# Layer 0's FFN in a two-layer backbone: the first product's copy, the left sums, row loads and residual loads in another order

## The chip, the core and the metric

The kernel runs on one core of one Trainium2 chip. The metric is the device time of one execution in microseconds (us); the figure that counts is the median of the runs. All data are fp32. The engines are TensorE (PE: matmuls; its weight loads are listed apart as PEld), VectorE (DVE), ScalarE (ACT), GpSimd (POOL) and SyncE (SP, which issues nearly all DMAs here). Each engine executes its own instructions strictly in the order in which they were written, and an instruction that has to wait holds up all that stand behind it on its engine.

## The reference

Two layers act on 1024 latent and 256 context tokens of width 1024. Layer 0 mixes by pooling, layer 1 by attention; behind each stands a gated ConvFFN. Every sub-layer is a root-mean-square norm with shift, scale and gate taken from a conditioning vector `c` through `ada_w`:

```
sh1, sc1, g1, sh2, sc2, g2 = split(silu(c) @ ada_w[i] + ada_b[i], 6)
x = x + g1 * mixer(modulate(rmsnorm(x), sh1, sc1))
x = x + g2 * conv_ffn(modulate(rmsnorm(x), sh2, sc2))

def conv_ffn(h):                        # D_FF = 2816 = 22 x 128
    u = h @ w_up                        # (tokens, 5632)
    u = u[t-1]*cw[0] + u[t]*cw[1] + u[t+1]*cw[2] + cb
    a, v = split(u, 2)
    return (silu(a) * v) @ w_down
```

The context stream runs through the same weights with a modulation of its own.

## The kernel before

**Products.** To keep fp32 accuracy a product is made of three matmuls: each operand is split into a high part (line 162, a cast on ACT) and a low part (line 163, a subtraction on DVE or POOL), and `mm3` (lines 166 to 168) multiplies high by high, high by low and low by high. For the latents, the up and the down product of layer 0 are done in Strassen's manner, with 7 half-size products in place of 8, so sums of weights and of tokens have to be made beforehand.

**Before the FFN.** The residual stream after the pool mixer, `tm(i)` for 128 tokens each (i = 0 to 7 latent, 8 and 9 context), is normalised: `norm2(i)` writes `xh2[i]`, on ACT (line 484) or on DVE (line 486). `turn_h2` transposes a piece on PE (line 795), and ACT (line 804) and DVE (line 803) read the transposed piece from PSUM, applying scale and shift (columns of `mod`, made on DVE in line 340). Lines 442 and 443 finish the mixer's output for other tiles. Up to the middle of this stretch a scheduler orders the instructions by due times and its own estimates; behind `tc.manual_schedule()` the order is that of a list of due times alone: `acts` holds (time, function) pairs, and `play` writes them between the PE's items as the estimated PE time goes by.

**Token sums.** `t0_subs` (line 818, DVE) makes four sums of the latent tokens in place, `t0_hi` (line 821, ACT) casts each, `t0_lo` (line 824, DVE) makes its low part. The four lie as halves of two tensors (`feat0`).

**Up phase.** 22 steps j, each one a block of 128 gate and 128 value columns of `w_up`. A step j >= 2 has 7 latent products of 512 columns (numbered 1 to 7) and four of 256 columns for the context (Ga, Gb, Va, Vb), in the order 1, 6, 2, Ga, Gb, 5, 7, 3, Va, 4, Vb. Product 1's bank is copied to SBUF by ACT (line 755, "the copy"), and product 2 goes on accumulating in that bank, so product 2 waits for the copy. DVE adds the products up (line 710). The convolution of the latent gate is an `ident` on ACT (line 717), two taps on DVE (line 722) and a silu on ACT (line 726); the value has the ident and the taps; the context has both in a smaller form (256 columns). Line 733 multiplies gate and value and the result is stored to `g0_d[j]`. POOL makes the weight sums of the coming step (line 660) and low parts.

**Left sums.** For the down phase, sums of pairs of `w_down` blocks (stored to `tw0_d`) and of pairs of gated blocks (stored to `sg0_d`) are made by groups of two loads (line 593), four DVE operations (line 590) and two stores (line 596). Of the 22 groups one falls to each up step from j = 3 on, and 3 are left for the beginning of the down phase.

**Down phase.** The context product goes first (22 blocks f, each with 4 `mm3`, some 2.7 us), then products 1, 6, 2 and so on with 11 blocks each. Each block's weights and gated values are loaded by SP (lines 947 and 951) into a ring of 4 buffers, cast by ACT, and their low parts are made by DVE or POOL. In the same time SP loads 24 row blocks of layer 1's `ada_w` (line 1023, 512 KB each) into a ring of 6; 16 of them are multiplied on PE by `c` (line 1033), 8 on DVE. The context's output leaves its banks on DVE (line 994) after its residual has been loaded (line 984). The first row group on PE (line 1033) writes a bank that line 994 has to read first.

Of the kernel before, what the change touches and what calls it, by code (L numbers as in the profile page):

```python
# [20 lines left out]
KT = D // P  # L21
LAT = 1024
# [60 lines left out]
def backbone(ctx: ExitStack, tc: tile.TileContext, io, out: bass.AP):  # L83
# [465 lines left out]
    on(73, lambda: rstd_of(0, 4))  # L549
    on(73.1, *(lambda i=i: norm2(i, True) for i in range(4)))  # L550

# [57 lines left out]
    def side_sums(w_dn, g_d, tw_d, sg_d, swap):  # L609
# [15 lines left out]
    w_up0 = io["ffn_w_up"][0].rearrange("(k p) f -> p k f", p=P)  # L625
    feat0 = {0: at(176, KT, 512), 512: at(192, KT, 512)}
    flo0 = {0: at(176, KT, 512, r=True), 512: at(192, KT, 512, r=True)}
    t_f32 = (feat0[0][:, :HK], feat0[512][:, HK:], feat0[512][:, :HK], feat0[0][:, HK:])
    t_sp = [(at(o, HK, 512, r=True), lo) for o, lo in
            zip((136, 104, 144, 96), (flo0[0][:, :HK], flo0[512][:, HK:], flo0[512][:, :HK], flo0[0][:, HK:]))]  # L630

# [103 lines left out]

    def ctx_acts(j, tg, tv):
        r = timed(tg, (0.1, 0.6, 1.0, 1.5), conv_ops(0, j, 0, csc[0], ctx_ps(j, 0), CTX))
        r += timed(tv, (0.1, 0.6, 1.0), conv_ops(0, j, 1, csc[1], ctx_ps(j, 1), CTX))
        return r + [(tv + 1.6, lambda: gated(j, *csc, LAT))]

    def lat_acts(j, t12, t21, tg, silu=3.8):
# [3 lines left out]
        r += timed(t21, (0.9, 1.9, 2.9), conv_ops(0, j, 1, cs[1], psum[:, v : v + LAT], LAT))  # L745
        return r + [(tg, lambda: gated(j, *cs, 0))]

    def up0_acts(j, end):
        b = banks0(j)
        b0, b1, bx, b2, b3 = (bank(n) for n in (b[1], b[3], 6, 4, 5))  # L750
        t12 = max(end[j, 3], end[j, 5] + 0.75) + 0.05
        t21 = max(end[j, 4] + 0.05, t12 + 2.85)
        tg = max(t21 + 4.1, end.get((j + 1, 6), 0) + 0.1)
        sums = [
            (end[j, 1] - 0.06, lambda: nc.scalar.copy(s1c0[j % 2], b0)),
            (end[j, 6], lambda: plus(vsum0, bx, s1c0[j % 2])),
            (end[j, 5], lambda: plus(rsum0, bx, s1c0[j % 2])),
            (end[j, 7], lambda: plus(b3, b2, rsum0)),
            (t12, lambda: plus(b1, b1, rsum0)),
            (t21, lambda: plus(b2, b2, vsum0)),  # L760
        ]
        return sums + lat_acts(j, t12, t21, tg) + ctx_acts(j, end[j, "Gb"], end[j, "Vb"])

# [27 lines left out]
    def turn_h2(o, kt, pt):  # L791
        n = 512 if o < LAT else CTX
        a = o // P
        for q in range(n // P):
            nc.tensor.transpose(pt[:, q * P : (q + 1) * P], xh2[a + q][:, kt * P : (kt + 1) * P], ident)
        s = 0 if o < LAT else 1
        sc, sh = mod[:, 0, 4, s, kt : kt + 1], mod[:, 0, 3, s, kt : kt + 1]
        hi, lo = h2_at(o, kt)
        f = feat0[o][:, kt] if o < LAT else hfr()
# [13 lines left out]
    def t0_subs(q):  # L813

        b11, b21 = feat0[0][:, q], feat0[0][:, HK + q]
        b12, b22 = feat0[512][:, q], feat0[512][:, HK + q]
        for o, x, y in ((b11, b12, b11), (b12, b22, b12), (b22, b22, b11), (b21, b21, b22)):
            nc.vector.tensor_tensor(out=o, in0=x, in1=y, op=ALU.subtract)
# [53 lines left out]
    for j, p in order:  # L872
        put(step0(j, p), j, p)
    acts = [(1, lambda: rstd_of(4, NLT))] + [(2, lambda i=i: norm2(i, i > 5)) for i in range(4, NLT)]

# [4 lines left out]
    for j, t in ((0, end0), (1, end1)):  # L880
        acts += ctx_acts(j, end[j, "Gb"], end[j, "Vb"]) + lat_acts(j, t - 0.7 + 1.3 * j, t - 0.7, t + 4 + 6 * j, 3.8 + 4.5 * j)
    acts += [(t_raw + 0.1 * n, lambda op=op: w0_make(1, op)) for n, op in enumerate(PLAIN)]
# [22 lines left out]

    for j in range(3, NJ):
        acts += sums0_acts(j - 3, end[j - 1, 7] + 0.1, end[j, 6] + 0.15, 0.01, end[j, 6] + 7)

# [1020 lines left out]
```

## Time and profile before

| | us |
|---|---|
| median of three runs (2240.66, 2245.22, 2245.85) | 2245.22 |
| the profiled execution | 2237.87 |
| its span, from first to last instruction | 2235.7 |
| PE busy in the span (10972 matmuls) | 2150.6 (96%) |
| DVE / POOL / ACT busy | 1514.5 / 1333.7 / 1000.6 |

Matmuls overlap, so PE's lost time is read from the distances of their starts. The chain of work that ended last gives PE 51%, DVE 21%, ACT 8% and POOL 7% of the span. By stage: the tokens' norm and transposes run from about 90 to 152 us, the up phase of layer 0 from there to about 690, its down phase to about 1000, layer 1 after that.

### The profile page before, as it was taken

What the parts mean: (1) busy time and instruction counts of PE and PEld (TensorE: products, weight loads), DVE (VectorE), ACT (ScalarE), POOL (GpSimd) and SP (SyncE); (2) the same over time, 40 slices, a digit from 0 to 9 for tenths busy, and PEclk for the clock granted to TensorE, in tenths of its full rate; (3) what the DMA queues carried; (4) which work ended last, traced back from release to release, by engine and by line L of the source; (5) the groups of instructions that cost most, each with busy time, mean ns of one, the idle gap of its engine ahead of it and who ended that gap; (6) DMA issues with size and microseconds to landing.
All of it is one profiled execution on the core that took longest, in us unless ns stands there. A gap on an engine that the chain in (4) does not pass through costs nothing.

```text
span 2235.7 us, 30177 instructions
## 1 busy us (share of the span) xinstructions
PE 2150.6 (96%) x10972; PEld 1768.7 (79%) x10972; DVE 1514.5 (68%) x2097; ACT 1000.6 (45%) x1589; POOL 1333.7 (60%) x881
## 2 busy tenths in 40 slices
PE   6899999999999899999998999989999999999999
PEld 5677888888887677887876877878878888888887
DVE  6666776777768657687776666746766666667565
ACT  5364333333335343454446665644443433444442
POOL 0444777677773267773345776734487777774755
PEclk9999999999999999999999999999999999999999
DMA  9832445444447998651000212123145555559775
GB/s 330 309 99 78 149 156 167 144 139 146 160 157 246 341 319 288 203 180 59 33 22 10 76 57 75 49 76 95 57 139 191 191 189 189 193 198 326 248 241 183
DMA packets 213927, 363.78 MB, mean 163 GB/s; under 512 B 15106, under 2 KB 114066, under 8 KB 213778
## 3 DMA queue, kind: packets, MB, share of 16 engines
q1 hardware_dynamic: 213778, 361.85, 47.7%
q8 instruction: 86, 1.41, 0.3%
q14 instruction: 63, 0.52, 0.1%
HBM read 271.86 MB, written 89.93 MB: 162 GB/s over the span
## 4 chain that ended last, share of the span: by engine, by line
PE 51%; DVE 21%; issue 8%; ACT 8%; POOL 7%; DMA 4%; SPq 0%; ACTq 0%; POOLq 0%; DVEq 0%
PE psum L166 15%; PE psum L167 15%; PE psum L168 15%; DVE a L722 5%; DVE a L590 5%; POOL a_512r L163 3%; PE psum L1390 3%; ACT a L717 2%; POOL a L660 2%; ACT a_512r L162 2%; DVE a_512r L163 1%; DVE a L1372 1%; DVE a L1217 1%; DVE a L733 1%; PE psum L315 1%
## 5 line engine op out<-in xcount | busy, mean ns | idle before, releaser
L163 POOL TENSOR_TENSOR a_512r<-a,a_512r 128x512 fp32r<-128x512 f32 x353 | 521.9, 1490 | 374.6 <-ACT a_512r L162 372.6
L162 ACT CAST a_512r<-a 128x512 fp32r<-128x512 f32 x507 | 294.2, 618 | 427.3 <-POOL a L660 200.7
L166 PE MATMUL psum<-a_2048r,a_512r 128*128 128x256 f32 (+1 forms) x1120 | 400.3, 358 | 7.1 <-DVE a L722 2.9
L168 PE MATMUL psum<-a_2048r,a_512r 128*128 128x256 f32 (+1 forms) x1120 | 399.0, 356 | 0.0
L167 PE MATMUL psum<-a_2048r,a_512r 128*128 128x512 f32 (+1 forms) x800 | 274.9, 344 | 0.0
L163 DVE TENSOR_TENSOR a_512r<-a,a_512r 128x512 fp32r<-128x512 f32 x154 | 180.6, 1182 | 110.7 <-ACT a_512r L162 108.5
L166 PEld LDWEIGHTS psum<-a_2048r,a_512r 128*128 128x128 f32 x1120 | 212.4, 190 | 41.0 <-DVE psum L1631 2.9
L166 PE MATMUL psum<-a_512r 128*128 128x512 f32 x616 | 242.9, 394 | 0.0
L167 PE MATMUL psum<-a_512r 128*128 128x512 f32 x616 | 240.5, 390 | 1.4 <-POOL a_512r L163 1.4
L168 PE MATMUL psum<-a_512r 128*128 128x512 f32 x616 | 240.2, 390 | 0.0
L722 DVE SCALAR_TENSOR_TENSOR a<-psum,conv,a 128x255 f32<-128x255 f32 (+1 forms) x176 | 150.6, 877 | 128.2 <-ACT a L717 126.6
L168 PEld LDWEIGHTS psum<-a_2048r,a_512r 128*128 128x128 f32 x1120 | 212.3, 190 | 30.4
L167 PE MATMUL psum<-a_4096r,a_512r 128*128 128x512 f32 x596 | 233.3, 391 | 0.0
L167 PEld LDWEIGHTS psum<-a_2048r,a_512r 128*128 128x128 f32 x800 | 152.2, 190 | 19.5
L168 PE MATMUL psum<-a_4096r,a_1024r 128*128 128x512 f32 x408 | 159.7, 392 | 1.5 <-POOL a_1024r L163 1.5
L166 PE MATMUL psum<-a_4096r,a_1024r 128*128 128x512 f32 x408 | 161.2, 395 | 0.0
L167 PE MATMUL psum<-a_4096r,a_1024r 128*128 128x512 f32 x408 | 159.5, 391 | 0.0
L1650 DVE SCALAR_TENSOR_TENSOR a<-psum,conv,a 128x1023 f32<-128x1023 f32 x88 | 112.9, 1283 | 58.9 <-ACT a L1642 57.4
L163 DVE TENSOR_TENSOR a_512r<-psum,a_512r 128x512 fp32r<-128x512 f32 x160 | 109.5, 690 | 50.6 <-ACT a_512r L162 49.3
L166 PEld LDWEIGHTS psum<-a_512r 128*128 128x128 f32 x616 | 115.9, 188 | 30.7 <-issue 6.2
L162 ACT CAST a_512r<-psum 128x512 fp32r<-128x512 f32 x160 | 92.1, 583 | 100.7 <-PE psum L1390 100.7
L1382 POOL TENSOR_SCALAR a<-a,stt 128x1280 f32<-128x1280 f32 x64 | 86.0, 1345 | 85.4 <-DVE stt L1381 74.5
(257 smaller groups left out, 4826.0 us busy)
## 6 DMA issues: line engine op xcount, KB each, us to landing
a<-in_ada_w_dram SPq DMA_DIRECT2D x96, 512.0 KB, 6.5
a<-in_ffn_w_up_dram SPq DMA_DIRECT2D x88, 512.0 KB, 5.8
a<-in_ffn_w_down_dram SPq DMA_DIRECT2D x66, 512.0 KB, 4.4
g_d<-a SPq DMA_DIRECT2D x44, 512.0 KB, 2.6
tw_d<-a SPq DMA_DIRECT2D x44, 512.0 KB, 3.0
a<-g_d SPq DMA_DIRECT2D x44, 512.0 KB, 4.4
sg_d<-a SPq DMA_DIRECT2D x44, 512.0 KB, 3.6
a<-tw_d SPq DMA_DIRECT2D x88, 256.0 KB, 3.9
```

The source lines that it names most:

```text
L162: nc.scalar.copy(hi, src)
L163: (lo_eng or nc.gpsimd).tensor_tensor(out=lo, in0=src, in1=hi.bitcast(F32), op=ALU.subtract)
L166: nc.tensor.matmul(ps, lh, rh, start=first, stop=False, skip_group_check=shared)
L167: nc.tensor.matmul(ps, lh, rl, start=False, stop=False, skip_group_check=shared)
L168: nc.tensor.matmul(ps, ll, rh, start=False, stop=last, skip_group_check=shared)
L590: return lambda: nc.vector.tensor_tensor(out=o, in0=x, in1=y, op=op)
L660: nc.gpsimd.tensor_tensor(out=o, in0=x, in1=y, op=f)
L717: nc.scalar.activation(dst, src, AF.Identity, scale=cv[:, 1, f : f + 1], bias=cv[:, 3, f : f + 1])
L722: nc.vector.scalar_tensor_tensor(out=dst[:, lo:hi], in0=src[:, lo + d : hi + d], scalar=cv[:, t, f : f + 1], in1=dst[:, lo:hi], op0=ALU.mu ...
L1382: nc.gpsimd.tensor_scalar(out=pb, in0=pb, scalar1=s_[:, 2:3], scalar2=1.0, op0=ALU.mult, op1=ALU.mult)
L1390: nc.tensor.transpose(pt[:, h * P : (h + 1) * P], probs[(4 * u + h) % len(probs)][:, k * P : (k + 1) * P], ident)
L1650: nc.vector.scalar_tensor_tensor(out=c[:, lo:hi], in0=psum[:, o + lo + d : o + hi + d], scalar=cv[:, t, f : f + 1], in1=c[:, lo:hi], op0=A ...
```

## The change

1. `norm2` of tiles 0 to 3 goes from ACT to DVE, and from the scheduler's list to the list of the FFN.
2. The four token sums lie in four tensors of their own.
3. In an up step the value's ident comes behind the copy of product 1 of the next step; all that hangs on it goes later with it. For the context of j = 1 the silu comes behind that copy too.
4. The groups of left sums begin at j = 2, so two are left for the down phase (at base + 8 and + 23 in place of + 8, + 24 and + 40), with the weights' last group now within the up phase.
5. The row blocks of `ada_w` have due times of their own, spread over the context product and products 1, 6 and 2, where before six were due near the end of the context product and each further one followed the use of an earlier one. The second row group on PE is due 1 us earlier.
6. The context's four residual loads are spread over the context product. Block 3 of the down phase is prepared 2.1 us earlier in the list.

```diff
-    on(73.1, *(lambda i=i: norm2(i, True) for i in range(4)))
+    acts = [(0.1 + 0.3 * i, lambda i=i: norm2(i)) for i in range(4)] + [...]
-    feat0 = {0: at(176, KT, 512), 512: at(192, KT, 512)}
+    feat0 = {0: [at(o, HK, 512) for o in (176, 184)], 512: [at(o, HK, 512) for o in (192, 200)]}
...
-        tg = max(t21 + 4.1, end.get((j + 1, 6), 0) + 0.1)
+        value = max(end.get((j + 1, 1), 0) - t21, 0.9)
+        tg = max(t21 + value + 3.2, end.get((j + 1, 6), 0) + 0.1)
...
-        r += timed(t21, (0.9, 1.9, 2.9), conv_ops(0, j, 1, cs[1], ...))
+        r += timed(t21, (value, value + 1, value + 2), conv_ops(0, j, 1, cs[1], ...))
...
+    sums0.insert(NH2 - 1, sums0.pop())
-    for j in range(3, NJ):
-        acts += sums0_acts(j - 3, end[j - 1, 7] + 0.1, end[j, 6] + 0.15, 0.01, end[j, 6] + 7)
+    for j in range(2, NJ):
+        acts += sums0_acts(j - 2, end.get((j - 1, 7), end1 + 2) + 0.1, end[j, 6] + 0.15, 0.01, end[j, 6] + 7)
...
-    acts += [(base + 22 * 4 * T3 - 17 + 4.2 * q, lambda q=q: ada_load(q)) for q in range(6)]
-        acts.append((t + 2.7 * (n == 1), lambda k=n + ahead_: d0_next(k)))
+        acts.append((t + 0.6 * (n == 1), lambda k=n + ahead_: d0_next(k)))
...
-        acts += [(ndone["ctx"] - 8, lambda i=i, half=half: x0_get(i, half)),
+        acts += [(ndone["ctx"] - 46 + 9 * q, lambda i=i, half=half: x0_get(i, half)),
...
-    for n in range(3):
-        t = base + 8 + 16 * n
-        acts += sums0_acts(NJ - 3 + n, t, t + 13, 0.9, t + 17, ...)
+    for n, t in ((NJ - 2, base + 8), (NJ - 1, base + 23)):
+        acts += sums0_acts(n, t, t + 11, 0.9, t + 15, ...)
+    t = ndone["ctx"]
+    at_ = [t - 34, t - 26, t - 18, t - 10, t - 3, t + 3, t + 7, t + 11] + [ndone[1] - 8 + 6.5 * m for m in range(KT)]
+    at_ += [ndone[2] - 14 + 2.6 * m for m in range(6)] + [ndone[2] + 6.1 + 2 * m for m in range(2)]
+    acts += [(t, lambda n=n: ada_load(n)) for n, t in enumerate(at_)]
```

Below, a row names the line, the operation, the tensor written and those read; `a36864_1024_286` is the buffer at offset 36864 with 1024 columns. The changed kernel's lines are numbered one to three lower.

ACT in an up step, before: `a32768` is the latent gate, `a36864` the latent value, `a137216` and `a138240` the context's gate and value.

```order
L717 ACTIVATE a32768_1024_285<-psum_124,conv0_114 128x1024
L162 CAST a212992_512r_275<-a172032_1024_138 128x512
L726 ACTIVATE a32768_1024_285<-a32768_1024_285 128x1024
L717 ACTIVATE a36864_1024_286<-psum_124,conv0_114 128x1024
L717 ACTIVATE a138240_256_288<-psum_124,conv0_114 128x256
L162 CAST a217088_512r_277<-a131072_512_279 128x512
L755 COPY a135168_512_282<-psum_124 128x512
```

The same stretch of ACT in the changed kernel:

```order
L714 ACTIVATE a32768_1024_289<-psum_124,conv0_114 128x1024
L162 CAST a212992_512r_279<-a172032_1024_138 128x512
L723 ACTIVATE a32768_1024_289<-a32768_1024_289 128x1024
L714 ACTIVATE a138240_256_292<-psum_124,conv0_114 128x256
L162 CAST a217088_512r_281<-a131072_512_283 128x512
L754 COPY a135168_512_286<-psum_124 128x512
L714 ACTIVATE a36864_1024_290<-psum_124,conv0_114 128x1024
```

The latent value's ident has gone from ahead of the context's ident, a cast and the copy to behind them.

DVE at the start of the FFN's token work, before: `st` holds the norms' statistics, `mod` the shift and scale columns.

```order
L178 SCALAR_TENSOR_TENSOR st_121<-st_121 128x4
L340 TENSOR_TENSOR mod_117<-psum_124,cols_113 128x2x4 x2
L442 TENSOR_TENSOR a143360_1024_195<-psum_124,a98304_1024_187 128x1024
L803 TENSOR_SCALAR a124928_256_249<-psum_124,mod_117 128x256
L803 TENSOR_SCALAR a122880_256_247<-psum_124,mod_117 128x256
L442 TENSOR_TENSOR a139264_1024_194<-psum_124,a98304_1024_187 128x1024
```

The same place on DVE in the changed kernel:

```order
L178 SCALAR_TENSOR_TENSOR st_121<-st_121 128x4
L486 TENSOR_SCALAR a114688_1024_191<-a180224_8192_125,st_121 128x1024
L486 TENSOR_SCALAR a118784_1024_192<-a180224_8192_125,st_121 128x1024
L486 TENSOR_SCALAR a126976_1024_193<-a180224_8192_125,st_121 128x1024
L486 TENSOR_SCALAR a102400_1024_188<-a180224_8192_125,st_121 128x1024
L340 TENSOR_TENSOR mod_117<-psum_124,cols_113 128x2x4 x2
L442 TENSOR_TENSOR a143360_1024_195<-psum_124,a98304_1024_187 128x1024
L442 TENSOR_TENSOR a139264_1024_194<-psum_124,a98304_1024_187 128x1024
L802 TENSOR_SCALAR a124928_256_249<-psum_124,mod_117 128x256
L802 TENSOR_SCALAR a122880_256_247<-psum_124,mod_117 128x256
```

Four norms now stand ahead of the columns, and both mixer sums ahead of the first reads of transposed context.

SP in the context product, before, from the second group's last load (the first is the row above it) to block 17's:

```order
L593 DMA a147456_1024_189<-g0_d21_80 128x1024
L596 DMA sg0_d9_90<-a98304_1024_187 128x1024
L596 DMA sg0_d9_90<-a102400_1024_188 128x1024
L947 DMA a163840_1024_136<-in_ffn_w_down_dram 128x1024
L951 DMA a110592_256_1169<-g0_d16_75 128x256
L947 DMA a167936_1024_137<-in_ffn_w_down_dram 128x1024
L951 DMA a111616_256_1170<-g0_d17_76 128x256
```

SP in the changed kernel, from the first group's store to block 16's loads:

```order
L595 DMA sg0_d9_90<-a98304_1024_187 128x1024
L592 DMA a106496_1024_196<-g0_d10_69 128x1024
L592 DMA a147456_1024_189<-g0_d21_80 128x1024
L1022 DMA a32768_1024_289<-in_ada_w_dram 128x1024
L595 DMA sg0_d9_90<-a102400_1024_188 128x1024
L946 DMA a176128_1024_139<-in_ffn_w_down_dram 128x1024
L950 DMA a113664_256_1172<-g0_d15_74 128x256
L946 DMA a163840_1024_136<-in_ffn_w_down_dram 128x1024
L950 DMA a110592_256_1169<-g0_d16_75 128x256
```

The group's loads and stores stand one block earlier, and the first row block of `ada_w` has come among them.

## Rows read from the trace of the kernel before

**Rows 1.** Timeline of PE at two copies: start, duration, instruction, [idle before <-releaser].

```profile
574.68 0.50 PE L166 MATMUL psum<-a_4096r,a_512r 128*128 128x512 f32 x1
...
599.24 0.39 PE L167 MATMUL psum<-a_4096r,a_512r 128*128 128x512 f32 x1
599.47 0.39 PE L168 MATMUL psum<-a_2048r,a_512r 128*128 128x512 f32 x1
600.00 0.50 PE L166 MATMUL psum<-a_4096r,a_512r 128*128 128x512 f32 x1
600.33 0.39 PE L167 MATMUL psum<-a_4096r,a_512r 128*128 128x512 f32 x1
```

**Rows 2.** Line 755, the copy: who waited for it (total us, times).

```profile
  PEld psum L166: 10.2, 16
```

**Rows 3.** Waits of PE, 183 to 700: total us, times, longest.

```profile
PE psum L166 <- DVE a L722: 2.9, 3, 1.2
PE psum L166 <- ACT a L755: 2.0, 2, 1.8
```

**Rows 4.** Timeline of ACT at the second copy.

```profile
597.30 1.64 ACT L717 ACTIVATE a<-psum,conv 128x1024 f32<-128x1024 f32 x2
...
599.35 0.59 ACT L755 COPY a<-psum 128x512 f32<-128x512 f32 x1
```

**Rows 5.** Timeline of DVE in the same step.

```profile
598.98 2.07 DVE L722 SCALAR_TENSOR_TENSOR a<-psum,conv,a 128x255 f32<-128x255 f32 x3 [2.13 <-ACT a L717]
601.08 1.39 DVE L733 TENSOR_TENSOR a<-a,a 128x256 f32<-128x256 f32 x1
602.40 1.27 DVE L722 SCALAR_TENSOR_TENSOR a<-psum,conv,a 128x1023 f32<-128x1023 f32 x1
...
605.32 1.78 DVE L590 TENSOR_TENSOR a<-a,a 128x512 f32<-128x512 f32 x1
607.13 0.69 DVE L590 TENSOR_TENSOR a<-a 128x512 f32<-128x512 f32 x1
```

**Rows 6.** Timeline of ACT at the token sums.

```profile
163.66 7.33 ACT L821 CAST a_2048r<-a 128x2048 fp32r<-128x2048 f32 x4 [11.66 <-DVE a L818]
```

**Rows 7.** Timeline of DVE at the token sums.

```profile
169.21 8.90 DVE L824 TENSOR_TENSOR a_4096r<-a,a_2048r 128x2048 fp32r<-128x2048 f32 x4 [4.92 <-ACT a_2048r L821]
```

**Rows 8.** Timeline of ACT at the norms.

```profile
105.69 4.27 ACT L484 ACTIVATE a<-a,st 128x1024 f32<-128x1024 f32 x4 [0.70 <-DVE st L178]
```

**Rows 9.** Line 486, a norm on DVE: duration min/median/max in ns, first and last start.

```profile
L486 DVE TENSOR_SCALAR a<-a,st x2: 748/750/753, 120.2 to 120.8; 128x1024 f32<-128x1024 f32 x2
```

**Rows 10.** Timeline of DVE at the norms.

```profile
103.25 2.40 DVE L178 SCALAR_TENSOR_TENSOR st<-st 128x4 f32<-128x4 f32 x1
...
105.72 1.21 DVE L442 TENSOR_TENSOR a<-psum,a 128x1024 f32<-128x1024 f32 x1
```

**Rows 11.** Timeline of POOL at the same place.

```profile
103.22 2.40 POOL L443 TENSOR_TENSOR a<-a,a 128x1024 f32<-128x1024 f32 x1 [1.92 <-DVE st L177]
```

**Rows 12.** Timeline of PE at the first context transposes.

```profile
112.54 1.28 PE L795 MATMUL psum<-ident,a 128*128 128x128 f32 x3 [4.12 <-ACT a_2048r L804]
```

**Rows 13.** Waits of PE, 700 to 1000.

```profile
PE psum L1033 <- DVE a L994: 3.9, 1, 3.9
PE psum L166 <- ACT a_1024r L162: 1.5, 1, 1.5
...
PE psum L167 <- POOL a_1024r L163: 1.3, 1, 1.3
```

**Rows 14.** Windows: length, busy PE, PEld, DVE, ACT, POOL, PEclk, DMA share, GB/s.

```profile
772.60:776.10 3.50, 3.50 (x14) 2.21 (x15) 1.92 (x2) 1.37 (x3) 3.50 (x4) 0.51 1.05 398
776.10:785.00 8.90, 8.90 (x50) 6.14 (x49) 5.93 (x6) 4.23 (x8) 8.90 (x7) 1.00 1.04 411
```

**Rows 15.** Timeline of ACT ahead of the wait of line 1033.

```profile
770.59 1.14 ACT L162 CAST a_512r<-a 128x512 fp32r<-128x512 f32 x2 [4.22 <-DMA a<-g_d]
```

**Rows 16.** Timeline of DVE ahead of the wait of line 1033.

```profile
771.24 0.69 DVE L163 TENSOR_TENSOR a_512r<-a,a_512r 128x512 fp32r<-128x512 f32 x1 [1.75 <-ACT a_512r L162]
```

More of the change, by code (lines that the diff above doesn't have):

```diff
@@ L625, in backbone @@
     w_up0 = io["ffn_w_up"][0].rearrange("(k p) f -> p k f", p=P)
-    feat0 = {0: at(176, KT, 512), 512: at(192, KT, 512)}
[L627 to L630, printed above, removed]
+    feat0 = {0: [at(o, HK, 512) for o in (176, 184)], 512: [at(o, HK, 512) for o in (192, 200)]}
+    t_f32 = (feat0[0][0], feat0[512][1], feat0[512][0], feat0[0][1])
+    t_sp = [(at(o, HK, 512, r=True), at(f, HK, 512, r=True)) for o, f in zip((136, 104, 144, 96), (176, 200, 192, 184))]
     def half_of(o, q):
@@ L734, in gated, with ctx_acts, lat_acts @@
         nc.sync.dma_start(g0_d[j][:, a : a + n], c1)
-    def ctx_acts(j, tg, tv):
-        r = timed(tg, (0.1, 0.6, 1.0, 1.5), conv_ops(0, j, 0, csc[0], ctx_ps(j, 0), CTX))
+    def ctx_acts(j, tg, tv, silu=1.5):
+        r = timed(tg, (0.1, 0.6, 1.0, silu), conv_ops(0, j, 0, csc[0], ctx_ps(j, 0), CTX))
         r += timed(tv, (0.1, 0.6, 1.0), conv_ops(0, j, 1, csc[1], ctx_ps(j, 1), CTX))
-        return r + [(tv + 1.6, lambda: gated(j, *csc, LAT))]
-    def lat_acts(j, t12, t21, tg, silu=3.8):
+        return r + [(max(tv + 1.6, tg + silu + 0.1), lambda: gated(j, *csc, LAT))]
+    def lat_acts(j, t12, t21, tg, silu=3.8, value=0.9):
         g, v = 1024 * (j % 2), (6 if j == 1 else 4) * 512
@@ L744, in lat_acts @@
         r = timed(t12, (0.8, 1.8, 2.8, silu), conv_ops(0, j, 0, cs[0], psum[:, g : g + LAT], LAT))
-        r += timed(t21, (0.9, 1.9, 2.9), conv_ops(0, j, 1, cs[1], psum[:, v : v + LAT], LAT))
+        r += timed(t21, (value, value + 1, value + 2), conv_ops(0, j, 1, cs[1], psum[:, v : v + LAT], LAT))
         return r + [(tg, lambda: gated(j, *cs, 0))]
@@ L761, in up0_acts @@
         ]
-        return sums + lat_acts(j, t12, t21, tg) + ctx_acts(j, end[j, "Gb"], end[j, "Vb"])
+        return sums + lat_acts(j, t12, t21, tg, value=value) + ctx_acts(j, end[j, "Gb"], end[j, "Vb"])
     def queue_up(j):
@@ L798, in turn_h2 @@
         hi, lo = h2_at(o, kt)
-        f = feat0[o][:, kt] if o < LAT else hfr()
+        f = feat0[o][kt // HK][:, kt % HK] if o < LAT else hfr()
         if kt % 2 and o < LAT:
@@ L813, in t0_subs @@
     def t0_subs(q):
-        b11, b21 = feat0[0][:, q], feat0[0][:, HK + q]
-        b12, b22 = feat0[512][:, q], feat0[512][:, HK + q]
+        b11, b21, b12, b22 = (h[:, q] for o in (0, 512) for h in feat0[o])
         for o, x, y in ((b11, b12, b11), (b12, b22, b12), (b22, b22, b11), (b21, b21, b22)):
@@ L873, in backbone @@
         put(step0(j, p), j, p)
-    acts = [(1, lambda: rstd_of(4, NLT))] + [(2, lambda i=i: norm2(i, i > 5)) for i in range(4, NLT)]
+    acts = [(0.1 + 0.3 * i, lambda i=i: norm2(i)) for i in range(4)] + [(1, lambda: rstd_of(4, NLT))] + [(2, lambda i=i: norm2(i, i > 5)) for i in range(4, NLT)]
     acts += [(t_man, lambda: ctx.enter_context(tc.manual_schedule()))]
@@ L880, in backbone @@
     for j, t in ((0, end0), (1, end1)):
-        acts += ctx_acts(j, end[j, "Gb"], end[j, "Vb"]) + lat_acts(j, t - 0.7 + 1.3 * j, t - 0.7, t + 4 + 6 * j, 3.8 + 4.5 * j)
+        acts += ctx_acts(j, end[j, "Gb"], end[j, "Vb"], max(1.5, j * (end[2, 1] - end[j, "Gb"]))) + lat_acts(j, t - 0.7 + 1.3 * j, t - 0.7, t + 4 + 6 * j, 3.8 + 4.5 * j)
     acts += [(t_raw + 0.1 * n, lambda op=op: w0_make(1, op)) for n, op in enumerate(PLAIN)]
@@ L1025, in ada_next @@
     def ada_next(n):
-        ahead = 6 if n < ADA0 else 2
-        if n + ahead < (ADA0 if n < ADA0 else len(ada_list)):
-            ada_load(n + ahead)
+        if ADA0 <= n < len(ada_list) - 2:
+            ada_load(n + 2)
     def ada_pe(n, b):
@@ L1034, in ada_pe @@
                              start=k == 0, stop=k == KT - 1, tile_position=(0, 32 * j))
-        ada_next(n)
     def ada_op(n):
@@ L1295, in backbone @@
         ]
-    for n in range(3):
-        t = base + 8 + 16 * n
-        acts += sums0_acts(NJ - 3 + n, t, t + 13, 0.9, t + 17, [at(o, 2, HC) for o in ((96, 100), (104, 144))[n % 2]])
+    for n, t in ((NJ - 2, base + 8), (NJ - 1, base + 23)):
+        acts += sums0_acts(n, t, t + 11, 0.9, t + 15, [at(o, 2, HC) for o in ((96, 100), (104, 144))[n % 2]])
     row1 = at(108, 256)
-    for u, n0, t, gap, b in ((0, 0, ndone["ctx"] + 4, 2.9, 0), (1, 2 * KT, ndone[2] + 7, 2, 2)):
+    t = ndone["ctx"]
+    at_ = [t - 34, t - 26, t - 18, t - 10, t - 3, t + 3, t + 7, t + 11] + [ndone[1] - 8 + 6.5 * m for m in range(KT)]
+    at_ += [ndone[2] - 14 + 2.6 * m for m in range(6)] + [ndone[2] + 6.1 + 2 * m for m in range(2)]
+    acts += [(t, lambda n=n: ada_load(n)) for n, t in enumerate(at_)]
+    for u, n0, t, gap, b in ((0, 0, ndone["ctx"] + 4, 2.9, 0), (1, 2 * KT, ndone[2] + 6, 2, 2)):
         acts += [(t + gap * k, lambda n=n0 + k, b=b: ada_pe(n, b)) for k in range(KT)]
```

## The prediction

> **What bounds the kernel now.** I read the stages first: PE is busy nearly all of the span, so time can only come from the places where it waits, and each has to be found by the distance of matmul starts. Then I asked PE's waits stage by stage, and where one repeats I followed the loop that makes it in the timelines of the other engines.
>
> In the up phase two copies lie 25.32 us apart on PE: it starts product 2 at 574.68 and again at 600.00 [rows 1]. In a steady stream two starts are 0.23 apart (599.24, 599.47); here the next comes 0.53 later and the one behind it 0.33 later. So 0.30 + 0.10 = 0.40 us of each such step is lost, and PE alone would need 24.92. The copy made PE's weight load wait 16 times [rows 2]. The loss is there in the steps from about 350 us on, 14 by my count; before that PE's early slack is used up. Beside these, PE waited for the convolution's taps 2.9 us in three places and for one late copy 1.8 [rows 3].
>
> What paces a step is a ring without PE in it: taps on DVE, silu and ident on ACT, the context's product and the left sums on DVE, casts on ACT, weight sums on POOL, and back to the gate's ident. The reader is to see in the ACT rows that the copy at 599.35 stands behind two idents that begin at 597.30 [rows 4], and in the DVE rows that DVE starts its three taps only at 598.98, because the context's ident is the second of the two [rows 5].
>
> In the down phase PE waited 3.9 us for line 994, 1.5 for a cast and 1.3 for a low part on POOL [rows 13]. Layer 1 isn't touched.
>
> **The change part by part**, made against the profiled execution of 2237.87 us. That lies 7.35 under the median of the runs shown, 2245.22; I take the gain to be the same in both.
>
> *The copy ahead of the value.* ACT does the same instructions: context ident, cast, copy, value ident. The context's ident now starts where the pair started, at 597.30; with 256 columns against 1024 it takes, as an estimate, about 0.5 of the pair's 1.64, leaving some 1.1 to 1.2 for the value. Its two taps can start at about 597.9 in place of 598.98, and end with the context product (1.39) at 600.2 at the latest. Meanwhile ACT has done the cast and the copy (0.59): the value's ident runs from about 598.9 to 600.0. Then two value taps of 1.27 each end at 602.6. Before, the second one ended at 602.40 + 1.27 = 603.67 [rows 5]. The ring is shortened by 1.0, to 24.3. What follows (vertical sum, four left sums, the latent product) is the same work in another order. 24.3 is less than PE's 24.92, so the copy no longer comes late, and what is late next is PE itself. Gain: 14 x 0.40 = 5.6. If the ring stays at PE's pace or above, nothing of it comes; if all 16 waits go, 6.4.
>
> *Four token tensors.* The first low part waits until 169.21 for the third cast [rows 7], though it needs the first, which ends at a quarter of 7.33 behind 163.66 [rows 6], at 165.5. The low parts move 3.7 us forward, and what hangs on them (the first gate taps, silu, POOL's first sums) with them. The early waits on taps, 1.2 and the next one, and the late copy, 1.8, are each less than 3.7; of the 2.9 I leave 0.9 for the last step, whose order isn't changed there. Gain: 2.0 + 2.0 = 4.0; bounds 2 and 4.9.
>
> *Norms on DVE.* ACT is freed of 4.27 us [rows 8], DVE gets four instructions of 0.75 [rows 9]. They stand behind line 178 (ends at 105.65) and ahead of the columns and of two mixer sums of 1.21 [rows 10], which the first reads of transposed context come behind. Line 178, a handful of elements, took 2.40 beside POOL's line 443 with its 2.40 [rows 10, 11]: DVE waits there for the POOL instruction that is running. POOL has low parts to make at this place. So the four take 3.0 if none meets POOL; beside POOL a left sum takes 1.78 in place of 0.69 [rows 5], and at 1.09 more each the four take 7.4. The reads come 2.4 behind them for the two of line 442, and some 0.7 more for the columns and the reads themselves (an estimate: a few hundred columns against the 1024 of line 442), so they end between 111.8 and 116.2. Before, PE resumed at 112.54, released by ACT [rows 12]. ACT's part is earlier now, so DVE's reads end last: PE resumes between 0.7 earlier and 3.7 later. I take 2.0 later, nearer to the row beside POOL.
>
> The Trainium skill, SBUF — State Buffer, "SBUF: two separate sides", says that DVE and GpSimd share one port pair as an exclusive lock, held for a whole instruction, for DVE operations with two SBUF inputs or in a 2-port mode. Lines 178 and 590 here agree. It speaks against this move: if the norms count as such operations the price would be the upper end, 3.7, and the sum 1.7 us worse.
>
> *The left sums of j = 2.* Four DVE instructions of 0.69 to 1.78 come into a step in which DVE's work ends 3.7 us earlier than before: hidden. Without that cover, 2.8 to 7.1 of DVE time and some of it on PE.
>
> *The down phase.* Line 1033 waited for line 994, which stands on DVE right behind a low part at 771.24; that one waited for ACT [rows 16], and ACT for a load of gated values that landed late [rows 15]. The group of left sums that ran there goes (2 MB of DMA, four DVE operations), three of four residual loads go ahead, and the row blocks are thinned out. The DMA engines were full there (share 1.05 and 1.04, 398 and 411 GB/s) [rows 14]. So the wait should go, and with it the stretch at half clock behind it: 3.5 us at 0.51, that is 1.7 [rows 14]. Of 3.9 + 1.7 = 5.6 I count 5.0; bounds 0 and 5.6. The wait of 1.3 for POOL [rows 13] goes: block 3's casts now stand ahead of the value's last ident. Bounds 0 and 1.3.
>
> The cast that PE waited 1.5 for belongs to block 16, behind the burst of the second group. This burst stays, and by order of SP a row block has come into it: 512 KB at 411 GB/s is 1.3 us more on queue. I count a loss of 1.3; bounds a gain of 1.5 (the group's earlier start helps) and a loss of 3.5 (residual loads as well, and a clock drop).
>
> Sum: -5.6 - 4.0 + 2.0 - 5.0 - 1.3 + 1.3 = -12.6. Profiled: 2225.3; on the median: 2232.6, rounded to 2232.
>
> **Rivals.** *The ring stays the bound.* Only 0.6 lies between 24.3 and 24.92. If DVE meets POOL once more per step (1.09), the ring is at 25.3 again, and the 5.6 don't come: -7.0, 2238. For it: DVE's operations are stretched wherever POOL works. Against it: the left sums already carry such waits in the 24.3.
>
> *The ring gets longer: slower.* The four left sums now stand ahead of the latent product, which the next gate's ident waits for. If two more of DVE's operations per step meet a POOL instruction, the ring is 24.3 + 2 x 1.09 = 26.4 at worst, 25.9 on average of one and a half: 0.6 us more in each of 20 steps, +12. With -4.0 + 2.0 - 5.0 for the rest: +5, 2250. It decides from a ring of 25.65, where 20 x 0.35 makes up for the 7.0 gained elsewhere. Against it: the ring has slack elsewhere, since ACT's casts wait for POOL and not for DVE.
>
> *The DMA side does not do what it says.* The burst moves and doesn't shrink: block 16 costs 3.5, and line 1033 still waits. Then -5.6 - 4.0 + 2.0 - 1.3 + 3.5 = -5.4, 2240. For it: the context product's loads alone fill most of the queue; against it: the worst full stretch came with the third group.
>
> **How the numbers follow.** Forecast 0.55, ring still the bound 0.17, DMA side 0.18, longer ring 0.10. About 0.3%, 6.7 us, is what a measurement can tell here, so faster means under 2238.5. The forecast is nearly all there (0.50), of the first rival half (0.08), of the third 0.07: faster 0.65. Same: 0.25. Slower: the longer ring, 0.10. All gains at their upper bounds give -6.4 - 4.9 - 0.7 - 5.6 - 1.3 - 1.5 = -20.4, 2225. The range goes from 2224 to 2243; 2 in 10 are left out, most of it above.
>
> **What would show it.** Copies 24.9 apart, with no gap on PE ahead of product 2, show the first step right; copies 25.3 or more apart with the gap show the ring. The first low part at 165.5 shows the second. PE's first transposes behind its idle time at about 114.5 show the norms' price; if the four norms take 0.75 each there, it is nought. No wait of line 1033, and a longer one ahead of block 16, show the down phase. The prediction is wrong if the copies stay 25.3 apart, or if a wait of several us stands in the down phase where none was.

## The result and the profile after

The changed kernel takes 2225.33 us, the median of 4 runs (2223.27 to 2228.45), against 2243.93 for the kernel before (4 runs, 2240.66 to 2245.85): a ratio of 0.992, with a 95% interval of 0.9902 to 0.9937. Run again beside the later experiments it took 2223.04 (6 runs) against 2240.29 (23 runs), 0.993 [0.9913, 0.9946]. So 17 to 19 us are gained, where 13 were forecast.

The profiled execution shows less: 2228.45, only 9.4 under the 2237.87 of before. To see why, compare the start of the same matmul in both traces. At 33 us of before the execution after was already 4.80 later, with the same instructions up to there in both kernels, and it is 4.82 later at 104, where the change begins. By 960 it is 12.2 earlier; in layer 1, which has not changed either, it loses 2.8 of that: between 1010 and 1300 the granted clock stood at 0.50 for 17 us, in before for 10. What belongs to the change is the part between, +4.82 to -12.2: 17.0 us. The second profile of the same kernel goes from -0.32 to -18.1 there, 17.8 us. This is the table by stage; a minus is time gained.

| Stage (before's time) | Forecast | after | again_after |
|---|---|---|---|
| 104 to 150, norms | +2.0 | +1.2 | +2.7 |
| 150 to 180, nothing changed | 0 | +1.6 | 0.0 |
| 180 to 204, token sums | -4.0 | -4.6 | -4.6 |
| 204 to 690, copies | -5.6 | -7.0 | -7.1 |
| 690 to 735, block 3 | -1.3 | -1.55 | -1.5 |
| 735 to 755, blocks 15 and 16 | +1.3 | +0.5 | -0.1 |
| 755 to 768, not in the sum | 0 | -1.4 | -1.4 |
| 768 to 782, line 1033 and the clock | -5.0 | -5.6 | -5.6 |

**The copies.** PE in the changed kernel, at the same two starts of product 2 as in [rows 1] (start, duration, instruction; a wait would stand in brackets):

```profile
573.45 0.39 PE L166 MATMUL psum<-a_4096r,a_512r 128*128 128x512 f32 x1
...
598.08 0.39 PE L168 MATMUL psum<-a_2048r,a_512r 128*128 128x512 f32 x1
598.31 0.39 PE L166 MATMUL psum<-a_4096r,a_512r 128*128 128x512 f32 x1
598.53 0.39 PE L167 MATMUL psum<-a_4096r,a_512r 128*128 128x512 f32 x1
```

They are 24.86 apart in place of 25.32, and the starts around product 2 follow each other at 0.23. The copy itself, now line 754, has the waiter of [rows 2] no more:

```profile
L754 ACT COPY a<-psum x20: 583/589/589, 198.0 to 670.4; 128x512 f32<-128x512 f32 x20
its engine sat idle before it (us, times) until:
  PE psum L168: 5.6, 7
who waited for it (us, times):
```

The list of those who waited is empty, and 7 times ACT was idle ahead of the copy, 5.6 us in all, until PE had finished product 1. ACT and DVE in that step, beside [rows 4, 5]:

```profile
595.25 0.55 ACT L714 ACTIVATE a<-psum,conv 128x256 f32<-128x256 f32 x1
595.70 0.61 ACT L162 CAST a_512r<-a 128x512 fp32r<-128x512 f32 x1
596.21 0.59 ACT L754 COPY a<-psum 128x512 f32<-128x512 f32 x1
596.69 1.22 ACT L714 ACTIVATE a<-psum,conv 128x1024 f32<-128x1024 f32 x1
```

```profile
595.83 1.00 DVE L719 SCALAR_TENSOR_TENSOR a<-psum,conv,a 128x255 f32<-128x255 f32 x2 [1.03 <-ACT a L714]
596.87 1.10 DVE L730 TENSOR_TENSOR a<-a,a 128x256 f32<-128x256 f32 x1
597.94 2.60 DVE L719 SCALAR_TENSOR_TENSOR a<-psum,conv,a 128x1023 f32<-128x1023 f32 x2
```

The context's ident takes 0.55, the copy ends 1.5 us ahead of product 2, and the taps of the value follow those of the context without idle time, though the value's ident now stands behind the copy.

**Token sums.** ACT's casts and the low parts that read them, the answer to [rows 6, 7]:

```profile
169.67 7.34 ACT L819 CAST a_2048r<-a 128x2048 fp32r<-128x2048 f32 x4 [11.63 <-DVE a L816]
```

```profile
171.62 8.90 DVE L822 TENSOR_TENSOR a_2048r<-a,a_2048r 128x2048 fp32r<-128x2048 f32 x4 [1.31 <-ACT a_2048r L819]
```

The first low part starts 1.95 behind the first cast, where it was 5.55. From 183 to 700 the list of PE's waits is empty; those of [rows 3], 4.9 us, are gone.

**Norms.** DVE, and POOL at the same time, beside [rows 8 to 11]:

```profile
108.06 2.41 DVE L178 SCALAR_TENSOR_TENSOR st<-st 128x4 f32<-128x4 f32 x1
110.51 5.75 DVE L486 TENSOR_SCALAR a<-a,st 128x1024 f32<-128x1024 f32 x4
...
116.33 2.34 DVE L442 TENSOR_TENSOR a<-psum,a 128x1024 f32<-128x1024 f32 x2
```

```profile
110.41 4.64 POOL L163 TENSOR_TENSOR a_512r<-a,a_512r 128x512 fp32r<-128x512 f32 x3
```

```profile
117.59 0.69 PE L794 MATMUL psum<-ident,a 128*128 128x128 f32 x2 [5.75 <-DVE a L442]
```

Four norms take 5.75, nearly twice four times the 0.75 of [rows 9], and PE is idle for 5.75 in place of the 4.12 of [rows 12], now released by DVE. It is not the same wait. Before made three transposes here in one go (first row below). Now the second and third of them wait, and start at 117.59, when the first of the two mixer sums from 116.33 on is done. The group that had waited in [rows 12] comes later, without a wait of its own (second row, from after):

```profile
106.75 0.67 PE L795 MATMUL psum<-ident,a 128*128 128x128 f32 x3
```

```profile
120.07 1.12 PE L794 MATMUL psum<-ident,a 128*128 128x128 f32 x4
```

With the 4.82 of the two traces' start taken off, 120.07 is 115.25, against 112.54 before: 2.7 later.

**The down phase.** The waits of PE from 700 to 1000, beside [rows 13], and windows (columns as in [rows 14]):

```profile
PE psum L166 <- ACT a_1024r L162: 1.9, 1, 1.9
PE psum L167 <- DVE a_1024r L163: 0.8, 1, 0.8
PE psum L1111 <- ACT a L1106: 0.4, 1, 0.4
PE psum L167 <- POOL a_512r L163: 0.4, 1, 0.4
```

```profile
735.00:739.00 4.00, 2.71 (x7) 1.97 (x8) 3.42 (x5) 3.19 (x5) 0.00 (x0) 0.77 1.01 392
760.00:776.00 16.00, 16.00 (x91) 10.89 (x90) 10.52 (x10) 6.70 (x12) 16.00 (x11) 1.00 0.86 294
```

The row of line 1033 and that of block 3's low part are missing. The stretch from 760 to 776, in which line 1033 had waited and the clock had fallen, is full of work at full clock, and its DMA share is 0.86 where it was above 1. What remains is a wait of 1.9 for a cast and of 0.8 for a low part behind it, at a DMA share of 1.01. It is not the wait of block 16 in before. A block of the context product is 12 matmuls, and with blocks numbered from 0 the 193rd matmul is the first of block 16; before waited there (first row), after at the 181st, the first of block 15 (second row, and ACT's cast for it):

```profile
743.27 0.50 PE L166 MATMUL psum<-a_1024r,a_256r 128*128 128x512 f32 x1 [1.45 <-ACT a_1024r L162]
```

```profile
735.53 0.50 PE L166 MATMUL psum<-a_1024r,a_256r 128*128 128x512 f32 x1 [1.93 <-ACT a_1024r L162]
```

```profile
734.13 0.40 ACT L162 CAST a_256r<-a 128x256 fp32r<-128x256 f32 x1 [7.96 <-DMA a<-g_d]
```

Block 16 waits no more. ACT was idle 7.96 until block 15's gated values had landed; in SP's new order their load stands right behind the second group's loads, the row block and the first group's last store.

### The profile page after: what moved, and what is told of

It is laid out like the page before. It is cut to its first block, busy times and chain, and to the rows that moved or that the text cites. A ratio compares the mean times of both kernels' runs of the same rounds, so it can differ in the third digit from the quotient of the medians.

```text
span 2226.3 us, 30135 instructions
## 1 busy us (share of the span) xinstructions
PE 2151.0 (97%) x10972; PEld 1775.5 (80%) x10972; DVE 1528.4 (69%) x2101; ACT 1000.1 (45%) x1585; POOL 1325.5 (60%) x881
## 3 DMA queue, kind: packets, MB, share of 16 engines
q8 instruction: 86, 1.41, 0.2%
## 4 chain that ended last, share of the span: by engine, by line
PE 75%; DVE 10%; ACT 4%; issue 4%; POOL 3%; DMA 3%; SPq 0%; ACTq 0%; POOLq 0%; DVEq 0%
PE psum L166 23%; PE psum L167 23%; PE psum L168 23%; PE psum L1389 2%; POOL a_512r L163 2%; DVE a L1371 1%; DVE a L1214 1%; DVE a_512r L163 1%; PE psum L315 1%; DMA a<-g_d 1%; ACT a L1376 1%; PE psum L396 1%; DVE a L1119 1%; ACT a_512r L162 1%; DVE hs L1181 1%
## 5 line engine op out<-in xcount | busy, mean ns | idle before, releaser
L163 POOL TENSOR_TENSOR a_512r<-a,a_512r 128x512 fp32r<-128x512 f32 x353 | 530.6, 1514 | 366.9 <-ACT a_512r L162 309.7
L166 PE MATMUL psum<-a_2048r,a_512r 128*128 128x256 f32 (+1 forms) x1120 | 399.4, 357 | 4.1 <-DVE psum L1630 2.4
L167 PE MATMUL psum<-a_2048r,a_512r 128*128 128x256 f32 (+1 forms) x1120 | 399.0, 356 | 0.0
L168 PE MATMUL psum<-a_2048r,a_512r 128*128 128x256 f32 (+1 forms) x1120 | 398.3, 356 | 0.0
L166 PEld LDWEIGHTS psum<-a_2048r,a_512r 128*128 128x128 f32 x1120 | 211.8, 189 | 37.0 <-DVE psum L1630 2.8
L167 PEld LDWEIGHTS psum<-a_2048r,a_512r 128*128 128x128 f32 x1120 | 211.6, 189 | 31.1 <-issue 0.4
L168 PEld LDWEIGHTS psum<-a_2048r,a_512r 128*128 128x128 f32 x1120 | 211.5, 189 | 30.2
L166 PEld LDWEIGHTS psum<-a_512r 128*128 128x128 f32 x616 | 115.6, 188 | 29.9 <-issue 5.4
L168 PEld LDWEIGHTS psum<-a_512r 128*128 128x128 f32 x616 | 115.6, 188 | 24.4
```

Source lines behind the costliest of these rows:

```text
L163: (lo_eng or nc.gpsimd).tensor_tensor(out=lo, in0=src, in1=hi.bitcast(F32), op=ALU.subtract)
L166: nc.tensor.matmul(ps, lh, rh, start=first, stop=False, skip_group_check=shared)
L167: nc.tensor.matmul(ps, lh, rl, start=False, stop=False, skip_group_check=shared)
L168: nc.tensor.matmul(ps, ll, rh, start=False, stop=last, skip_group_check=shared)
```

## The experiments

The parts have the numbers of the section on the change. The kernels were run in three batches, each with its own runs of the kernel before: 2239.93 us for e1 to e4, 2240.07 for e5, e7 and the two of e8, 2240.29 for the rest.

**e1_copy: before, with part 3 alone.** Its core:

```diff
-        tg = max(t21 + 4.1, end.get((j + 1, 6), 0) + 0.1)
+        value = max(end.get((j + 1, 1), 0) - t21, 0.9)
+        tg = max(t21 + value + 3.2, end.get((j + 1, 6), 0) + 0.1)
```

> The kernel before with the copy's order alone (part 3: the value's ident behind the copy). Theory (a ring through DVE, ACT and POOL paces the step): copies come 24.9 us apart in place of 25.3, the 14 to 16 gaps of 0.40 us ahead of product 2 are gone, gain 5.6 to 7 us; the early waits for the taps (1.4 and 0.9 us near 183 and 192) stay. Rival (the steps were late only because the token sums let them start late): copies stay 25.3 us apart, gain 0 to 2 us.

2229.82 (6 runs), 0.9946 [0.993, 0.9962].

```profile
L756 ACT COPY a<-psum x20: 584/587/600, 192.8 to 665.3; 128x512 f32<-128x512 f32 x20
...
who waited for it (us, times):
```

20 copies from 192.8 to 665.3 are 24.87 apart on the mean, and nobody waits for one. The steps from 205 to 690 give 7.3 us, with the early start of the token work unchanged. So the order on ACT alone removes the gaps; that a late start had caused them falls. The early waits for the taps, which I had expected to stay, are 0.6 in place of 2.9; PE came 1.6 us later to the first of them, behind a stretch at half clock (150 to 180).

**e2_tokens: before, with part 2 alone.** Its core:

```diff
-    feat0 = {0: at(176, KT, 512), 512: at(192, KT, 512)}
+    feat0 = {0: [at(o, HK, 512) for o in (176, 184)], 512: [at(o, HK, 512) for o in (192, 200)]}
```

> The kernel before with the four token tensors alone (part 2). Theory (ring): the first low part starts some 3.7 us earlier behind the casts, the early waits near 183, 192 and 197 go, but copies stay 25.3 us apart, only the gaps begin some 9 steps later (3.7 us of lead at 0.4 us a step): gain about 4 us. Rival (late start is all): the gaps ahead of product 2 vanish too, copies 24.9 us apart, gain 9 to 11 us.

2235.67 (12 runs), 0.9982 [0.9972, 0.9993]: 4.3 us.

```profile
L753 ACT COPY a<-psum x20: 577/592/594, 198.2 to 676.6; 128x512 f32<-128x512 f32 x20
...
  PEld psum L166: 7.1, 13
```

The early waits go, 4.6 us in the trace between 180 and 205; one of 0.9 at the last step is left. But 20 copies in 198.2 to 676.6 are still 25.18 apart on the mean, 25.29 from the fifth on, and the weight loads wait for 13 of them. The gaps came back sooner than I had expected.

**e3_down: before, with parts 4 to 6.** The edits are those of the diff from `sums0.insert` on.

> The kernel before with the down phase's parts alone (left sums from j = 2, row blocks and residual loads spread, block 3 earlier; parts 4 to 6). Theory (loads that land late behind the third group's burst hold up line 994): the wait of 3.9 us of line 1033 and the half clock behind it go, the 1.3 us wait for block 3's low part goes, block 16 still waits some 2 us: gain 6 to 9 us. Rival (the DMA queue is full anyway, thinning out only moves the wait): line 1033 or a block of product 1 still waits 3 us or more, gain under 3 us.

2230.20 (7 runs), 0.9956 [0.9941, 0.9972].

```profile
PE psum L166 <- ACT a_1024r L162: 1.0, 1, 1.0
PE psum L167 <- DVE a_1024r L163: 0.8, 1, 0.8
...
```

These are the longest two of PE's waits from 700 to 1000: the wait of line 1033 is gone, and those for block 15 are there, as in after. From 690 to 781 the trace gains 9.0 us. At 205 it is 1.3 us behind its place at 183, which looked like the price of the left sums of j = 2 without cover; e9_sums and e10_rows, below, show that it isn't.

**e4_norms: before, with part 1 alone.**

```diff
-    on(73.1, *(lambda i=i: norm2(i, True) for i in range(4)))
+    acts = [(0.1 + 0.3 * i, lambda i=i: norm2(i)) for i in range(4)] + [...]
```

> The kernel before with the four norms on DVE alone (part 1). Theory (they meet POOL's low parts): the four take 5 to 7 us on DVE, PE's idle time ahead of the second group of transposes is 5.5 to 6 us in place of 4.1, and the kernel is 1 to 3 us slower. Rival (ACT's relief pays for it): the four take 3 us, PE resumes as early as before or earlier, and the kernel is the same or up to 2 us faster.

2243.17 (12 runs), 1.0014 [1.0002, 1.0025]: slower by about 3 us. The waits of PE from 100 to 183:

```profile
PE psum L794 <- DVE a L442: 5.8, 1, 5.8
PE psum L794 <- ACT a_2048r L803: 3.6, 4, 1.4
```

The norms cost time by themselves, as a wait for DVE's mixer sums.

**e5_no_norms: after without part 1.** The reverse of that diff.

> The changed kernel with the four norms back on ACT (part 1 undone). Theory (the norms on DVE cost what they cost alone, and nothing later makes use of ACT's relief): PE's idle time ahead of the second transposes is about 4.1 us again, 2 to 3.5 us faster than the changed kernel's 2225.3. Rival (the relief of ACT is what lets the rest work, for instance the token sums): the same or slower than the changed kernel.

2220.57 (4 runs), 0.9913 [0.9899, 0.9926].

```profile
113.50 1.50 PE L794 MATMUL psum<-ident,a 128*128 128x128 f32 x4 [4.11 <-ACT a_2048r L803]
```

PE's idle time is that of [rows 12] again, with ACT as its releaser. The ratio lies under the 0.992 of after with overlapping intervals. The sign is clear from all traces together: against before, the stage from 104 to 150 takes 1.2 to 3.9 us more in the six with part 1, and between 1.2 less and nothing more in the seven without it.

**e7_burst: after, with the first row block and the second group further apart.**

```diff
-    for n, t in ((NJ - 2, base + 8), (NJ - 1, base + 23)):
-        acts += sums0_acts(n, t, t + 11, 0.9, t + 15, ...)
-    at_ = [t - 34, ...
+    for n, t in ((NJ - 2, base + 6), (NJ - 1, base + 25)):
+        acts += sums0_acts(n, t, t + 11, 0.9, t + 14, ...)
+    at_ = [t - 43, ...
```

> The changed kernel with the burst ahead of block 16 drawn apart: the first row block 9 us earlier, the first group's loads 2 us and its stores 3 us earlier, the second group's loads 2 us later. Theory (block 16 waits because some 2.5 MB stand ahead of its loads on one queue): PE's wait there falls from 2.1 us to under 1, and the half clock behind it goes: 2 to 4 us faster than the changed kernel's 2225.3. Rival (the loads of the context product alone fill the queue and the ring of four buffers sets the pace): a wait of 2 us or more stays, there or at a later block, and the time is within 1 us of the changed kernel's.

2220.96 (4 runs), 0.9914 [0.9899, 0.9928]. The longest wait of PE from 700 to 1000:

```profile
PE psum L167 <- DVE a_1024r L163: 0.5, 1, 0.5
...
```

No wait is longer than this one, for block 17's low part. The wait for block 15's cast is gone; from 735 to 782 the trace gains 3.3 us on after and 2.8 on again_after, the stretch at 0.77 in the window above among them. ACT's longest wait for a load of the context product is now this:

```profile
701.55 0.41 ACT L162 CAST a_256r<-a 128x256 fp32r<-128x256 f32 x1 [4.28 <-DMA a<-g_d]
```

It is 4.28 here and 4.72 in e13_best, which has the same edit, and 7.3 to 8.1 in the six traces of the changed down phase without it (after, again_after, e3_down, e5_no_norms and the two of e8). So the loads queued ahead of block 15's make that load late. Whether PE waits depends on when it gets there, too: in both runs of e8, where the up phase takes longer, the load is as late and PE doesn't wait for the cast. By the medians alone the gain on after is not clear of noise.

**e8_ring1 and e8_ring2: after, with the vertical sum done two and three times,** so some 0.7 and 1.4 us more of DVE in each step, where I had expected 0.6 and 1.2 (two of these sums take 1.41 in the trace, one 0.69; the repeats write the same values).

```diff
             (end[j, 6], lambda: plus(vsum0, bx, s1c0[j % 2])),
+            (end[j, 6], lambda: plus(vsum0, bx, s1c0[j % 2])),
```

> The changed kernel with one sum of an up step (product 1 and 6 into the vertical sum, DVE, 128x512 out of PSUM) done twice: 0.6 us more on DVE in each step, nothing else. Theory (the ring of DVE, ACT and POOL takes 24.35 to 24.4 us where it is free, PE 24.86): within the slack of 0.5, copies stay 24.9 us apart on average, 0 to 4 us slower. Rival (DVE is far from the bound): no difference at all, here and with two.

> The same with that sum done three times: 1.2 us more on DVE in each step. Theory: the ring is 25.5 to 25.6 us, above PE's 24.86, copies 25.5 us apart, gaps ahead of product 2 are back, 9 to 15 us slower than the changed kernel. Rival (DVE is far from the bound): copies stay 24.9 us apart, under 2 us slower.

2232.97 (5 runs), 0.9964 [0.9951, 0.9978], and 2239.04 (11 runs), 0.9992 [0.9984, 1.0001]. The copy of e8_ring1, and PE at one of them:

```profile
L754 ACT COPY a<-psum x20: 580/583/589, 198.6 to 680.6; 128x512 f32<-128x512 f32 x20
...
  PEld psum L166: 9.5, 14
```

```profile
655.24 0.39 PE L168 MATMUL psum<-a_2048r,a_512r 128*128 128x512 f32 x1
655.86 0.50 PE L166 MATMUL psum<-a_4096r,a_512r 128*128 128x512 f32 x1 [0.24 <-ACT a L754]
```

The pattern of [rows 1, 2] is back: copies 25.41 apart in the later steps, 14 late ones, 0.62 from one start to the next where 0.23 is the rule. The first repeat brings 0.55 a step over PE's 24.86, the second only 0.21 more (25.62). So what is put into the ring doesn't count in full, and how far it is under PE's pace stays open; it is less than the 0.6 that I had worked out.

**e9_sums and e10_rows: before, with part 4 alone and with part 5 alone.**

> The kernel before with the left sums alone begun at j = 2 (part 4): two groups left for the down phase. Theory (the third group's loads, stores and DVE operations are what makes line 994 late): the wait of line 1033 falls under 1 us, gain 4 to 6 us, less some 1.6 us that the four sums cost in step j = 2 while the token sums are late. Rival (the row blocks' loads fill the queue): line 1033 still waits 2 us or more, gain under 2 us.

> The kernel before with the row blocks of ada_w alone spread (part 5). Theory (the third group is the cause): line 1033 still waits 2 us or more, gain 0 to 2 us. Rival (the row blocks are the cause): the wait falls under 1 us, gain 4 to 6 us.

e9_sums: 2234.44 (12 runs), 0.9978 [0.9966, 0.9989]. e10_rows: 2240.21 (12 runs), 0.9997 [0.9986, 1.0007]. The waits of PE from 700 to 1000, first of e9_sums, then of e10_rows:

```profile
PE psum L1034 <- DVE a L995: 2.7, 1, 2.7
...
PE psum L167 <- POOL a_512r L163: 0.5, 1, 0.5
```

```profile
PE psum L167 <- POOL a_512r L163: 1.4, 2, 0.8
...
PE psum L166 <- ACT a_512r L162: 1.1, 1, 1.1
PE psum L1032 <- DVE a L994: 1.1, 1, 1.1
...
```

The wait of line 1033 is 2.7 without the third group and 1.1 with the row blocks spread, in place of 3.9. Two things forbid reading prices off that. The same wait also moves in kernels whose down phase is untouched, here e1_copy and e2_tokens:

```profile
PE psum L1034 <- DVE a L995: 4.0, 1, 4.0
```

```profile
PE psum L1030 <- DVE a L991: 2.4, 1, 2.4
```

And PE waits for casts and low parts of late gated values up to 10 us ahead of line 1033 (in e10_rows 1.1 and 0.8); what it has waited there it need not wait again. All waits between 755 and 782 of before's time together are 4.8 in before, 5.9 in e1_copy, 4.4 in e2_tokens and 6.2 in e4_norms, but 2.7 in e9_sums, 3.1 in e10_rows and none in e3_down. So each of the two edits takes away a part, neither account holds alone, and how they share it isn't shown. That the two suffice isn't shown either: e3_down and after spread the residual loads as well (part 6), and no run has parts 4 and 5 without that.

In the medians the third group counts for more, 5.9 us (interval 2.5 to 7.6) against 0.1 (from 3.1 faster to 1.6 slower) for the row blocks. Of e9_sums' gain 1.4 us lie near 765, in a wait that the forecast had not counted. Another 3.0 lie at block 16, whose wait for its cast is missing, and with it the half clock behind; but it is missing in e2_tokens too, with the old down phase, so that isn't shown to be the group's doing.

These two also settle the step j = 2. e9_sums has its four left sums and loses nothing between 183 and 205; e10_rows hasn't, and is 1.3 later there, as e3_down is. So that loss is not the left sums'. It is the clock: behind the same wait of 1.8 for the copy the granted clock was 0.50 for 3.4 us in e3_down (from 201.3 on) and e10_rows (from 203.5 on), and 1.00 in before and e9_sums.

**again_after and e13_best.** e13_best joins the two edits that helped: after without part 1, with the diff of e7_burst.

> The changed kernel once more beside the others: ratio to the kernel before 0.992 as at first, between 0.990 and 0.994.

> The changed kernel with both: the four norms back on ACT and the burst ahead of block 16 drawn apart. Theory (the two losses are in different places and add up): 1.2 us of PE's idle time at the norms and 3.3 us at block 16 go, 3 to 5 us faster than the changed kernel run beside it. Rival (they share a cause, or what one gives back the other loses): no faster than the better of the two, 1 to 2 us.

again_after: 2223.04 (6 runs). e13_best: 2218.46 (4 runs, 2215.33 to 2220.21), 0.9902 [0.9887, 0.9918], 4.6 us under after in the same batch, and 21.8 under before: it beats both kernels. Its slowest run is faster than the fastest of again_after (2221.36). No wait of PE from 700 to 1000 is longer than 0.5.

## Why the prediction was right

The time lies within the range, and the largest steps came by the mechanism that was told: the copies, the token tensors, line 1033. Two steps came another way, the norms and block 16, and a wait was passed over. By the traces the sum was too small by 4 to 5 us, spread over several terms. That the range held is partly luck: 2225.33 lies 1.3 above its lower end, about where all gains at their upper bounds had been put (2225). The base was off too: the 2245.22 of three runs is 5 above the 2240.29 of the 23 later ones.

- **The copies.** Right as a mechanism, shown by e1_copy, which has this edit alone. The term of 5.6 measured 7.0: 6.2 in the steps themselves, nearer to the upper bound of 6.4 with all 16 of [rows 2] than to the 14 counted, and 0.8 at the last step, whose wait I had left standing. What was mis-sized behind it is the ring, 24.3 with 0.6 to spare: in e8_ring1 some 0.7 us of DVE more makes the step longer by 0.55, where 0.6 to spare would have left 0.1. The rival in which the ring stays the bound was nearer than its 0.17 said.
- **The token tensors.** The term of 4.0 measured 4.6. The low part moved 3.6 forward, as worked out (3.7), and it hid the waits of [rows 3] but the last step's, as I had it. By itself it gave 4.3 in e2_tokens.
- **The norms.** +2.0 was taken between -0.7 and +3.7. The group of [rows 12] came 2.7 later in both profiles of the changed kernel, on before's time at 115.25 where about 114.5 was the sign. But the path was another: PE stopped one group of transposes earlier, for the first mixer sum, and not for DVE's reads of transposed context. Of the 2.7, 1.2 to 2.7 was left at 150, and e4_norms lost 3.2 in the median (interval 0.4 to 5.6). The four took 5.75, between the 3.0 of a free engine and the 7.4 beside POOL, because POOL's three low parts covered 4.6 us of it. The Trainium skill, SBUF — State Buffer, "SBUF: two separate sides", has DVE and GpSimd take turns at a shared port pair under an exclusive lock; these durations agree, 0.74 for a norm alone and up to 1.75 here. The upper end of the forecast, 3.7, was not reached.
- **The left sums of j = 2.** Hidden, as forecast. The price without cover, 2.8 to 7.1, is not shown: e9_sums has no earlier token work and lost nothing.
- **Line 1033 and the half clock.** The term of 5.0 measured 5.6, its upper bound. The cause was rightly placed on the loads: without the third group and with the other loads spread, the wait is gone in every trace. How much of it belongs to which of them stays open.
- **Block 3.** 1.3 was forecast, 1.55 came.
- **Block 16.** This step failed in its place. I let the burst stay ahead of block 16 and grow there by a row block. In the changed order it stands ahead of block 15: block 16's wait went, and block 15 waited 1.9 (1.4 in the second profile). So the longer wait ahead of block 16, which was to show the down phase, never came, and since the new wait is about as long as the old one, the net price was 0.5 and -0.1 in place of 1.3. e7_burst shows that what is left there is nearly all avoidable.
- **Not in the sum.** A wait near 764 for a low part of gated values, 0.9 in the list and 1.4 by the distance of starts, went with the third group. It is part of the line left out between the rows of [rows 13] (POOL a_512r, 1.4 in two places): I passed over it.

Of the rivals, the longer ring fell with e1_copy. The third fell as well: line 1033 waits no more.

## What to carry to other kernels

Where PE waits again and again for a short instruction in another engine's queue, look for a longer one ahead of it whose result is wanted later: that exchange gave the largest part here. Before work goes from one engine to another, look at what POOL does at that time; four instructions of 0.75 cost 5.75 beside it. Where a wait has two suspects on one queue, take each away alone and both together, and look first how far the wait moves in kernels that leave it alone: here from 2.4 to 4.0. And count which matmul waits, in both traces, before a wait that is still there is called the same one.

## What the runs showed of the hardware

The clock did not do the same in two executions of the same kernel. After a wait of 1.35 us at the same place, with the same work ahead of it and behind, the granted clock was 0.50 (1.2 GHz) for 3.2 us in the profile of after and 1.00 (2.4 GHz) in that of again_after:

```profile
154.00:156.90 2.90, 1.55 (x11) 1.22 (x12) 1.97 (x3) 2.83 (x5) 0.98 (x1) 0.99 0.00 0
156.90:160.10 3.20, 3.20 (x9) 2.55 (x8) 1.93 (x3) 1.14 (x2) 1.53 (x2) 0.50 0.00 0
```

```profile
150.30:153.20 2.90, 1.55 (x11) 1.23 (x11) 2.01 (x3) 2.82 (x5) 0.93 (x1) 1.00 0.00 0
153.20:156.40 3.20, 3.20 (x15) 2.63 (x14) 1.88 (x3) 1.19 (x2) 1.61 (x2) 1.00 0.00 0
```

The same 3.2 us hold 9 matmuls in the one and 15 in the other; that is the 1.6 us in the second line of the table. Seven of the fourteen traces lose 1.5 to 1.6 us there and seven don't, with kernels of the old and of the new order in both groups. With the 4.80 us of the first 33 and the 2.8 of layer 1, such differences are why one pair of profiles gave half the gain that the medians show: a change of 0.5 to 1% is read between the same matmuls of both traces, and not from their ends.
